# Hybrid decoder layer on one core: ScalarE takes over the remaining threshold searches, four gate tiles are made in two passes, and the attention's pools change places

## The chip, the cores and the metric

One core of one Trainium2 chip runs the kernel. The metric is the device time of one execution in microseconds (us), the median of several runs. The five engines are PE (TensorE, the matmuls), DVE (VectorE), ACT (ScalarE), POOL (GpSimd) and SP (SyncE, whose queue issues nearly all DMAs here).

## The reference

Input x is 2048 tokens by 1024 channels, float32. Cut to what matters:

```
h = rms_norm(x);  P = h @ w_in        # conv parts, q, k, v, indexer iq, ik, iw, gates g_a, g_b
y_a = (B * causal_conv3(C * x_a)) @ w_branch_a
score[t,s] = sum_h iw[t,h] * relu(iq[t,h] . ik[s])            # causal
idx = top_k(score, 256)               # per query token
y_b = softmax(q . k[idx] + bias) @ v[idx]  ->  @ w_branch_b   # 8 heads
m = sigmoid(g_a) * y_a + sigmoid(g_b) * y_b
x = x + m @ w_out
x = x + swiglu(rms_norm(x))           # 1024 -> 2816 -> 1024
out = rms_norm(x)
```

## The kernel before, in words

Matmuls in full precision are made as three: an operand is split into a high part that the fast float32 format holds and the rest, and `mm3` (L154 to L157) multiplies high by high, high by low and low by high. The tokens stand in 4 chunks of 512, or 16 blocks of 128 (blocks 0 to 7 are chunks 0 and 1).

**Stage A** makes all projections. `proj` (L187) loads the weights of one tile of 128 columns (two DMAs of 256 KB, split into whi on ScalarE, L129, and wlo on GpSimd, L130) and does 24 matmuls for each chunk, with the chunks' transposed inputs hThi and hTlo. Between them it steps a generator of indexer scores (`score`, L250): for a block of queries and up to 512 keys, per head two matmuls into sc (L258, L259), a ReLU on ScalarE into a buffer r (L261, three buffers), and a multiply-add on VectorE into acc (L266). Finished scores go to DRAM (SD). After the queries and the indexer come six gate tiles, the convolution and ten more gate tiles (`evac_gate`, L508: tanh, then a store to GT).

**The searches.** For each block of queries from block 2 on, the value of the 256th largest score is found bit by bit. On VectorE (`descend`, L298) each bit is one count over all keys of the block (`count`, L285) and two tiny steps (L339 and L341, or the like for the upper bits); there are 33 counts. On ScalarE (`descend_act`, L373) each bit is one pass of Sign with a sum over the keys (L358), and two tiny steps (way, L367; nt, L369); there are 33 passes. Then `topk` (L418) makes the mask on VectorE (L425 to L447) and stores it to DRAM (MS); the attention loads it as Mt. `A_DVE` and `A_ACT` list the blocks searched in stage A by either engine, `C_ACT` those that ScalarE searches later, between attention 0 and attention 1. All searches have low priority: the tile scheduler puts their instructions where its own simulation has the engine free, and writes one fixed order for each engine and for SP's queue.

**The halves.** `attention(half)` (L559) handles blocks 7 to 0 in half 0 and blocks 15 to 8 in half 1, four heads at a time (head groups hg 0 and 1): logits (L629, L630), a reduction on VectorE that adds mask and bias and takes the maximum (L632), the exponential (L636), transposes (L676) into ph and pl, products with V (L663, L664), then t, which is copied from PSUM on ScalarE (L668), multiplied by the spread reciprocals R on GpSimd (L669), and stored to AT (L670). Its SBUF pools stack up as kv, ap, pr. The merge follows: w_branch_a and w_branch_b are loaded (L808) and split into wab, the conv output (YT) and AT are loaded (L779, L785), the gates are loaded (L828, L830). Then come w_out (dn<-o), the norm and the transposes into h2hi and h2lo (`norm_transpose`, L839; L147 to L150), and SwiGLU (L899 on). The pools of merge and SwiGLU reuse the bytes of the attention's pools, tile by tile: a load into such a tile waits for whatever last used its bytes.

```
A_ACT, A_DVE = (5, 6, 7, 8, 9, 10), (2, 3, 4)
C_ACT, C_DVE = (15, 14, 13, 12, 11), ()
```

Of the kernel before, what the change touches and what calls it, by code (L numbers as in the profile page):

```python
# [25 lines left out]
P = 128  # L26
# [20 lines left out]

A_ACT, A_DVE = (5, 6, 7, 8, 9, 10), (2, 3, 4)
C_ACT, C_DVE = (15, 14, 13, 12, 11), ()
ORDER = ((7, 6, 5, 4, 3, 2, 1, 0), (15, 14, 13, 12, 11, 10, 9, 8))  # L50
# [24 lines left out]
def trunk_kernel(tc, x, g_mix, w_in, b_gate, conv_w, w_a, w_b, w_out, rel_bias,  # L75
# [38 lines left out]
    bg = const.tile([P, 16], F32, name="bg")  # L114
    zero = edge.tile([P, 1], F32, name="zero")
    nc.gpsimd.memset(zero, 0.0)
# [133 lines left out]
    def score(b):  # L250
        iqb = iqp.tile([P, NH, P], F32R, name="iqb", tag="iqu", bufs=2)
        c, o = divmod(b * P, CH)
        nc.gpsimd.dma_start(out=iqb, in_=IQ[c][:, :, o:o + P].rearrange("h p t -> p h t"))
        for s0, w in cut((b + 1) * P):
            acc = tk.tile([P, CH], F32, name="acc", tag="acc", bufs=2)
            for h in range(NH):
                sc = scp.tile([P, CH], F32, name="sc", tag="sc")
                nc.tensor.matmul(sc[:, 0:w], iqb[:, h, :], IKH[:, s0:s0 + w], start=True, stop=False)  # L258
                nc.tensor.matmul(sc[:, 0:w], iqb[:, h, :], IKL[:, s0:s0 + w], start=False, stop=True)  # L259
                r = tk.tile([P, CH], F32, name="r", tag="r", bufs=3)  # L260
                nc.scalar.activation(r[:, 0:w], sc[:, 0:w], AF.Relu)  # L261
                wv = iwT[:, b, h:h + 1]
                if h == 0:
                    nc.vector.tensor_scalar(acc[:, 0:w], r[:, 0:w], wv, None, op0=ALU.mult)
                else:
                    nc.vector.scalar_tensor_tensor(acc[:, 0:w], r[:, 0:w], wv, acc[:, 0:w],  # L266
                                                   op0=ALU.mult, op1=ALU.add)
                yield
            if s0 + w == (b + 1) * P:
                nc.vector.tensor_tensor(acc[:, w - P:w], acc[:, w - P:w], cmin, op=ALU.min)  # L270
            nc.sync.dma_start(out=SD[b][:, s0:s0 + w], in_=acc[:, 0:w])
        if b in A_DVE:
            select_block(b)
        elif b in A_ACT:
            select_block_act(b)
# [15 lines left out]
    def parts(b):  # L291

        for s0, w in cut((b + 1) * P):
            S = TK["p"].tile([P, CH], F32, name="S", tag="S", bufs=2)
            nc.sync.dma_start(out=S[:, 0:w], in_=SD[b][:, s0:s0 + w])
            yield slice(s0, s0 + w), w, S[:, 0:w].bitcast(U16).rearrange("p (n e) -> p n e", e=2)

# [152 lines left out]
    def select_block(b):  # L450
        with tc.high_priority(offset=-LOW):
            topk(b, descend(b), wide("J"))

    def select_block_act(b):
        with tc.high_priority(offset=-LOW):
            thr = descend_act(b)
            topk(b, thr, TK["a"].tile([P, TK["alen"]], U8, name="dump", tag="dump", bufs=1).bitcast(BF16))

# [91 lines left out]
    for ch in range(4):  # L550
        conv_tile(ch)
    for j in range(6, 16):
        proj(C_GA + j * P, P, evac_gate(j))
    for _ in scores:
        pass
# [3 lines left out]
    def attention(half):  # L559
        b_stack = ExitStack()  # L560
        LH = (half + 1) * 1024
        kvp = pool(b_stack, f"kv{half}")
        ap = pool(b_stack, f"ap{half}")
        prp = pool(b_stack, f"pr{half}")
        lgp = pool(b_stack, f"lg{half}", bufs=LGB, space=PSUM)
# [24 lines left out]
        def setup(b):  # L590
# [15 lines left out]
            near = min(lw, 2 * P)  # L606
            MBs = [ap.tile([P, CH], F32, name="MB", tag="MB", bufs=4) for _ in range(2)]
            if lw > near:
# [5 lines left out]
        def logits(st, hg, res):  # L614

            b, n, q, Mt, spans, near, MBs = st
            lw = spans[-1][1]
            sums = ap.tile([P, 4], F32, name="sums", tag="sums", bufs=3)
            for hh in range(4):
# [3 lines left out]
                pr = prp.tile([P, LH], F32, name="pr", tag="pr", bufs=PRB[half])  # L623
                mx = ap.tile([P, 5], F32, name="mx", tag="mx", bufs=6)
                for i, (s0, w) in enumerate(spans):
# [12 lines left out]
                yield  # L638
            rec = ap.tile([P, 4], F32, name="rec", tag="rec", bufs=3)
            nc.vector.reciprocal(rec, sums)  # L640
            res.append(rec)

        def spread(b, hg, rec):

            tp = tpb.tile([P, CH], F32, name="tpb", tag="tpb")
            in_order(nc.tensor.transpose(tp[0:4, 0:P], rec, ident))
            row = ap.tile([4, P], F32, name="row", tag="row", bufs=2)
            nc.scalar.copy(row, tp[0:4, 0:P])
# [95 lines left out]
    for half in (0, 1):  # L744
        ends = attention(half)
        mc = ExitStack()
        if half == 0:
            search_pool(mc, "tkc", C_DVE, C_ACT, 4)
            TK["p"].tile([P, 16], F32, name="pad")
        bigp = pool(mc, f"bigp{half}", bufs=4)  # L750
# [119 lines left out]
        if half == 0:  # L870
            with tc.issue_after(ends[-1].ins):
                for b, ba in itertools.zip_longest(C_DVE, C_ACT):
                    if ba is not None:
                        select_block_act(ba)
                    if b is not None:
                        select_block(b)
        if half == 1:
# [104 lines left out]
```

## Time and profile before

| | |
|---|---|
| median of 3 runs | 3313.43 us (3310.44 to 3317.68) |
| the profiled execution | 3308.23 us |
| its span | 3306.3 us |
| mean granted TensorE clock | 0.990 |
| PE busy | 3206.5 us, 97% |
| VectorE busy | 1744.3 us, 53% |
| ScalarE busy | 1763.8 us, 53% |
| GpSimd busy | 774.4 us, 23% |

The span is the time from the first to the last instruction that the profile shows; the execution's time has some 2 us more around it. Times inside the trace count from the span's start. A share of busy time is a mean over stages that have different limits: stage A lasts to about 1004 us, attention 0 to about 1147, SwiGLU of half 0 to about 2078, attention 1 to about 2369.

### The profile page before, as it was taken

The page shows a single profiled execution, that of the slowest core. Times are in us where ns is not written, and L with a number is a line of the kernel's source. Part 1 is how long each engine was busy: PE and PEld are TensorE (multiplying, and loading weights), DVE is VectorE, ACT ScalarE, POOL GpSimd, SP SyncE. Part 2 cuts the span into 40 slices and gives each one's busy share as a digit, 9 for nine tenths or more (in the row PEclk, how much of TensorE's full clock was granted, in tenths as well). Part 3 has the DMA queues.
Part 4 walks back from the last instruction along what each step waited for, and adds up shares of the span by engine and source line. Part 5 has one row for each costly group of instructions (what it writes and reads, how often), then busy time and mean ns, then how long its engine had stood idle before and what let it go on. Part 6 is the DMA issues. An engine that isn't in the chain of part 4 may idle for free.

```text
span 3306.3 us, 41232 instructions
## 1 busy us (share of the span) xinstructions
PE 3206.5 (97%) x14723; PEld 2626.5 (79%) x14723; DVE 1744.3 (53%) x3422; ACT 1763.8 (53%) x3250; POOL 774.4 (23%) x684
## 2 busy tenths in 40 slices
PE   8999899999997899899999999999999999999999
PEld 6777788888886678788888888787787888888887
DVE  6389756565327775554535423898854422332234
ACT  6433478877877786867586611677632211111111
POOL 5411012221013520321221222222222222212221
PEclk9999999999999999999999999999999999999999
DMA  7643333333235692322212211422571411111111
GB/s 231 179 126 115 93 97 96 92 98 107 85 99 137 167 287 78 98 78 83 88 60 77 79 51 60 115 60 72 149 250 45 147 51 44 46 51 45 45 45 51
DMA packets 347077, 328.94 MB, mean 99 GB/s; under 512 B 20596, under 2 KB 276808, under 8 KB 346488
## 3 DMA queue, kind: packets, MB, share of 16 engines
q1 hardware_dynamic: 310248, 297.84, 29.4%
q0 software_dynamic: 36624, 28.48, 4.0%
q8 instruction: 115, 1.88, 0.2%
q14 instruction: 90, 0.74, 0.1%
HBM read 252.28 MB, written 75.54 MB: 99 GB/s over the span
## 4 chain that ended last, share of the span: by engine, by line
PE 79%; DVE 9%; DMA 5%; ACT 3%; issue 2%; POOL 1%; SPq 0%; POOLq 0%; DVEq 0%; ACTq 0%
PE gu L155 11%; PE gu L157 11%; PE gu L156 11%; PE mm L157 6%; PE mm L155 6%; PE mm L156 6%; PE dn L155 5%; PE dn L157 5%; PE dn L156 5%; PE tpb L676 3%; DVE J L285 2%; PE pv L663 2%; PE lg L629 1%; PE pv L664 1%; PE lg L630 1%
## 5 line engine op out<-in xcount | busy, mean ns | idle before, releaser
L155 PE MATMUL gu<-h2hi,wgu 128*128 128x512 f32 x1408 | 552.7, 393 | 0.0
L156 PE MATMUL gu<-h2lo,wgu 128*128 128x512 f32 x1408 | 552.1, 392 | 0.0
L157 PE MATMUL gu<-h2hi,wgu 128*128 128x512 f32 x1408 | 552.0, 392 | 0.0
L358 ACT ACTIVATE dump<-key,nt 128x768 uint8<-128x768 int16 (+21 forms) x330 | 484.2, 1467 | 8.4
L157 PE MATMUL mm<-hThi,wlo 128*128 128x512 f32 (+2 forms) x1216 | 471.7, 389 | 2.6 <-POOL wlo L130 2.5
L155 PE MATMUL mm<-hThi,whi 128*128 128x512 f32 (+2 forms) x1216 | 473.7, 390 | 0.4 <-ACT whi L129 0.4
L156 PE MATMUL mm<-hTlo,whi 128*128 128x512 f32 (+2 forms) x1216 | 471.1, 388 | 0.0
L937 DVE SCALAR_TENSOR_TENSOR x<-dn,x 128x512 f32<-128x512 f32 x352 | 241.7, 689 | 224.4 <-PE dn L157 224.3
L130 POOL TENSOR_TENSOR wlo<-raw,whi 128x512 fp32r<-128x512 f32 (+1 forms) x132 | 175.9, 1333 | 696.8 <-ACT whi L129 659.3
L156 PEld LDWEIGHTS gu<-h2lo,wgu 128*128 128x128 f32 x1408 | 265.2, 188 | 58.5
L157 PEld LDWEIGHTS gu<-h2hi,wgu 128*128 128x128 f32 x1408 | 265.0, 188 | 58.6
L155 PEld LDWEIGHTS gu<-h2hi,wgu 128*128 128x128 f32 x1408 | 265.2, 188 | 58.4
L130 POOL TENSOR_TENSOR hid<-th,hid 128x512 fp32r<-128x512 f32 x88 | 114.6, 1302 | 808.1 <-ACT hid L129 800.8
L266 DVE SCALAR_TENSOR_TENSOR acc<-r,iwT,acc 128x512 f32<-128x512 f32 (+2 forms) x266 | 196.1, 737 | 197.3 <-ACT r L261 196.6
L920 DVE SCALAR_TENSOR_TENSOR th<-th,gu 128x512 f32<-128x512 f32 x88 | 60.5, 687 | 432.5 <-ACT th L919 379.0
L130 POOL TENSOR_TENSOR wgu<-raw,wgu 128x1024 fp32r<-128x1024 f32 x88 | 216.6, 2462 | 271.5 <-ACT wgu L129 268.4
L155 PE MATMUL dn<-wd,hid 128*128 128x512 f32 x704 | 274.5, 390 | 0.0
L157 PE MATMUL dn<-wd,hid 128*128 128x512 f32 x704 | 274.1, 390 | 0.0
L156 PE MATMUL dn<-wd,hid 128*128 128x512 f32 x704 | 274.0, 389 | 0.0
L157 PEld LDWEIGHTS mm<-hThi,wlo 128*128 128x128 f32 (+1 forms) x1216 | 227.1, 187 | 54.5 <-POOL wlo L130 5.1
L155 PEld LDWEIGHTS mm<-hThi,whi 128*128 128x128 f32 (+1 forms) x1216 | 227.4, 187 | 44.1 <-ACT whi L129 1.7
L156 PEld LDWEIGHTS mm<-hTlo,whi 128*128 128x128 f32 (+1 forms) x1216 | 227.4, 187 | 42.9
(229 smaller groups left out, 5853.3 us busy)
## 6 DMA issues: line engine op xcount, KB each, us to landing
raw<-in_w_in_dram SPq DMA_DIRECT2D x124, 256.0 KB
raw<-in_w_ffn_gate_dram SPq DMA_DIRECT2D x44, 512.0 KB
raw<-in_w_ffn_up_dram SPq DMA_DIRECT2D x44, 512.0 KB
raw<-in_w_ffn_down_dram SPq DMA_DIRECT2D x44, 512.0 KB
S<-SD SPq DMA_DIRECT2D x80, 256.0 KB
GT<-f SPq DMA_DIRECT2D x64, 256.0 KB
ta<-GT SPq DMA_DIRECT2D x64, 256.0 KB
S<-SD SPq DMA_DIRECT2D x68, 192.0 KB
```

What stands on the lines that cost most here:

```text
L130: lo_eng.tensor_tensor(lo, raw, hi.bitcast(F32), op=ALU.subtract)
L155: nc.tensor.matmul(ps, whi, xhi, start=start, stop=False)
L156: nc.tensor.matmul(ps, whi, xlo, start=False, stop=False)
L157: nc.tensor.matmul(ps, wlo, xhi, start=False, stop=stop)
L266: nc.vector.scalar_tensor_tensor(acc[:, 0:w], r[:, 0:w], wv, acc[:, 0:w], op0=ALU.mult, op1=ALU.add)
L285: nc.vector.tensor_scalar(wide("J")[:, 0:n], xs, thr, None, op0=op, op1=ALU.add, accum_out=cnt)
L358: nc.scalar.activation(dump, keys, AF.Sign, bias=nt, accum_out=sm)
L629: in_order(nc.tensor.matmul(lg[:, o2:e2], q[:, h, :], KH[:, s0 + o2:s0 + e2], start=True, stop=False))
L663: in_order(nc.tensor.matmul(pv, V[:, sb, :], ph, start=sb == 0, stop=False))
L676: in_order(nc.tensor.transpose(tp[:, hh * P:(hh + 1) * P], Ps[hh][:, sb * P:(sb + 1) * P], ident))
L920: nc.vector.scalar_tensor_tensor(th, th, 1.0, g, op0=ALU.add, op1=ALU.mult)
L937: nc.vector.scalar_tensor_tensor(x2[tt][:, ns], ps, 0.5, x2[tt][:, ns], op0=ALU.mult, op1=ALU.add)
```

## The change

The diff below is cut to its core; from the attention on, line numbers of the changed kernel are eight higher.

- ScalarE searches blocks 2 to 9 in stage A, and VectorE none; block 10 moves to the later group (15, 14, 13, 12, 11, 10).
- In that group block 15 may start when the attention's last ph and pl are made, and its `topk` only after the last norm transpose; all others only after the last norm transpose. Before, all of them could start at the first of these points.
- The last four gate tiles (12 to 15) are made for chunks 0 and 1, then once more loaded and made for chunks 2 and 3.
- r has four buffers, the score parts S two in stage A and four in the later group.
- The attention's pools stack up as kv, mb (MB, sums, mx), pr, ap (ph, pl, R, t), few (rec, row).

```diff
-A_ACT, A_DVE = (5, 6, 7, 8, 9, 10), (2, 3, 4)
-C_ACT, C_DVE = (15, 14, 13, 12, 11), ()
+A_ACT, A_DVE = tuple(range(2, 10)), ()
+C_ACT, C_DVE = (15, 14, 13, 12, 11, 10), ()
...
-                r = tk.tile([P, CH], F32, name="r", tag="r", bufs=3)
+                r = tk.tile([P, CH], F32, name="r", tag="r", bufs=4)
...
-            S = TK["p"].tile([P, CH], F32, name="S", tag="S", bufs=2)
+            S = TK["p"].tile([P, CH], F32, name="S", tag="S", bufs=TK["eqs"])
...
-    def select_block_act(b):
-        with tc.high_priority(offset=-LOW):
+    def select_block_act(b, after=()):
+        with tc.high_priority(offset=-LOW), ExitStack() as stack:
             thr = descend_act(b)
+            for ins in after:
+                stack.enter_context(tc.issue_after(ins))
             topk(b, thr, TK["a"].tile([P, TK["alen"]], U8, name="dump", tag="dump", bufs=1).bitcast(BF16))
...
-    for j in range(6, 16):
+    for j in range(6, 12):
         proj(C_GA + j * P, P, evac_gate(j))
+    for chunks in ((0, 1), (2, 3)):
+        for j in range(12, 16):
+            proj(C_GA + j * P, P, evac_gate(j), chunks)
...
         kvp = pool(b_stack, f"kv{half}")
+        mbp = pool(b_stack, f"mb{half}")
+        mbp.tile([P, 56], F32, name="pad")
+        prp = pool(b_stack, f"pr{half}")
         ap = pool(b_stack, f"ap{half}")
-        prp = pool(b_stack, f"pr{half}")
+        few = pool(b_stack, f"few{half}")
...
             with tc.issue_after(ends[-1].ins):
-                for b, ba in itertools.zip_longest(C_DVE, C_ACT):
-                    if ba is not None:
-                        select_block_act(ba)
-                    if b is not None:
-                        select_block(b)
+                select_block_act(C_ACT[0], [transposed[-1].ins])
+            with tc.issue_after(transposed[-1].ins):
+                for b in C_ACT[1:]:
+                    select_block_act(b)
```

What the scheduler makes of it shows in the engines' fixed order. VectorE where stage A ends and attention 0 begins (L410 to L415 end a search, L425 to L447 are its topk, L632, now L640, are the attention's reductions), before:

```order
L410 TENSOR_SCALAR li<-nt 128x1
L413 TENSOR_TENSOR li<-li,turn 128x1
L415 TENSOR_TENSOR thr<-li,top 128x1
L425 SCALAR_TENSOR_TENSOR dump,cnt_7133<-S,thr,zerob 128x512 x2
L632 ISA pr,mx<-lg,Mt 128x512
L632 ISA mx 128x1
L431 TENSOR_TENSOR more<-cnt_7133 128x1
```

and after the change:

```order
L446 SCALAR_TENSOR_TENSOR eq<-S,thr,eq 128x384
L447 TENSOR_SCALAR eq<-eq 128x384
L441 TENSOR_SCALAR eq<-S,thr 128x384
L442 SCALAR_TENSOR_TENSOR cs<-eq,last 128x384
L444 CAST last<-cs 128x1
L445 SCALAR_TENSOR_TENSOR eq<-cs,need,eq 128x384
L446 SCALAR_TENSOR_TENSOR eq<-S,thr,eq 128x384
L447 TENSOR_SCALAR eq<-eq 128x384
L640 ISA pr,mx<-lg,Mt 128x512
L640 ISA mx 128x1
```

Before, the last search's end (block 10) and the head of its topk stand ahead of the first reduction, and the rest of that topk among the reductions. Now the last topk (block 9) stands whole ahead of the first reduction, and the last pass of that block on ScalarE comes ahead of the last nine of the gates' evacuations; before, block 10's last pass came behind all of them.

SP's queue where attention 0 ends and the merge begins, before (RD, R and AT<-t belong to the attention, the raw loads and ta to the merge, S<-SD to a search):

```order
L650 DMA RD_81<-row 4x128
L808 DMA raw_12250<-in_w_branch_a_dram 128x4x128
L650 DMA RD_82<-row 4x128
L808 DMA raw_12256<-in_w_branch_b_dram 128x4x128
L652 DMA R<-RD_81 128x512
L670 DMA AT_77<-t 128x4x128
L652 DMA R<-RD_82 128x512
L670 DMA AT_77<-t 128x4x128
L828 DMA ta<-GT_114 128x512
```

and after:

```order
L660 DMA R<-RD_82 128x512
L295 DMA S<-SD_148 128x512
L678 DMA AT_77<-t 128x4x128
L295 DMA S<-SD_148 128x512
L678 DMA AT_77<-t 128x4x128
L295 DMA S<-SD_148 128x512 x2
L793 DMA raw_12218<-AT_77 64x2x512
L678 DMA AT_77<-t 128x4x128
L793 DMA raw_12218<-AT_77 64x2x512
L793 DMA raw_12219<-AT_77 64x2x512 x2
L816 DMA raw_11935<-in_w_branch_a_dram 128x4x128
L816 DMA raw_11941<-in_w_branch_b_dram 128x4x128
```

The first load of w_branch_a has moved from ahead of the attention's last four stores to behind the last of them and behind four loads from AT. The same holds at the end of attention 1.

ScalarE at the norm transposes of half 0 (o<-x squares a token tile, h2hi evacuates transposes, L358 to L369 are a search), before:

```order
L135 ACTIVATE o_13676,ss<-x_12988 128x1024
L358 ACTIVATE dump,sm<-key,start_hi 128x1920
L367 ACTIVATE way<-sm 128x1
L369 ACTIVATE nt<-way,start_hi 128x1
L358 ACTIVATE dump,sm<-key,nt 128x1920
L149 ACTIVATE h2hi<-gu 128x4x128
L135 ACTIVATE o_13698,ss<-x_13037 128x1024
L149 ACTIVATE h2hi<-gu 128x4x128 x3
```

and after:

```order
L135 ACTIVATE o_13361,ss<-x_12673 128x1024
L149 ACTIVATE h2hi<-gu 128x4x128
L135 ACTIVATE o_13383,ss<-x_12722 128x1024
L149 ACTIVATE h2hi<-gu 128x4x128 x9
L129 ACTIVATE wd<-raw_15429 128x1024
```

Block 14's search stood among the transposes' evacuations; now its first pass comes behind all sixteen. The last search of the group ends ahead of the 39th of the 44 tanh of this SwiGLU, with block 10 in it; before, the last, block 11, ended ahead of the 32nd.

## Rows read from the trace of the kernel before

**Rows 1.** The page: the chain that ended last, its share by engine.

```profile
PE 79%; DVE 9%; DMA 5%; ACT 3%; issue 2%; POOL 1%; SPq 0%; POOLq 0%; DVEq 0%; ACTq 0%
```

**Rows 2.** Busy time by stretch: stage A, its first and its later part.

```profile
core 0: us, PE busy (x) PEld busy (x) DVE busy (x) ACT busy (x) POOL busy (x), PEclk, DMA share, GB/s
180.00:420.00 240.00, 224.42 (x981) 180.70 (x980) 203.56 (x592) 95.37 (x206) 28.57 (x23) 0.99 0.38 112
420.00:960.00 540.00, 539.38 (x2409) 449.28 (x2408) 289.00 (x533) 438.22 (x984) 92.25 (x73) 1.00 0.34 98
```

**Rows 3.** Waits, 180 to 440 us: total us, times, longest.

```profile
PE sc L258 <- ACT r L261: 13.2, 11, 6.5
```

**Rows 4.** Groups by line and shape, VectorE, whole span: count, busy, mean ns.

```profile
L285 DVE TENSOR_SCALAR_CACHE_REDUCE J<-up,l 128x512 bf16<-128x512 uint16 x16 | 11.9, 744 | 0.4
...
L341 DVE SCALAR_TENSOR_TENSOR l<-l,ldrop 128x1 f32<-128x1 f32 x48 | 11.3, 235 | 1.4
...
L339 DVE TENSOR_SCALAR ldrop<-cnt,more 128x1 f32<-128x1 f32 x48 | 10.2, 212 | 1.1
```

**Rows 5.** Groups by line and shape, ScalarE, whole span.

```profile
L369 ACT ACTIVATE nt<-way,nt 128x1 f32<-128x1 f32 x330 | 96.5, 292 | 8.2
...
L358 ACT ACTIVATION_READ_ACCUMULATOR dump<-key,nt 128x1 f32 x330 | 61.8, 187 | 0.0
...
L358 ACT ACTIVATE dump<-key,nt 128x1408 uint8<-128x1408 int16 x15 | 22.0, 1468 | 0.4
...
L358 ACT ACTIVATE dump<-key,nt 128x768 uint8<-128x768 int16 x15 | 14.0, 934 | 0.4
```

**Rows 6.** Timeline of PE where stage A ends and attention 0 begins.

```profile
1004.35 0.39 PE L157 MATMUL mm<-hThi,wlo 128*128 128x512 f32 x1
...
1015.54 0.80 PE L629 MATMUL lg<-KH,q 128*128 128x512 f32 x1 [9.44 <-DVE mx L632]
```

**Rows 7.** Timeline of VectorE in the same place.

```profile
1012.75 0.15 DVE L410 TENSOR_SCALAR li<-nt 128x1 int32<-128x1 f32 x1 [39.84 <-ACT nt L369]
```

**Rows 8.** Busy time by stretch (columns as in rows 2): attention 0, attention 1.

```profile
1020.00:1060.00 40.00, 33.47 (x180) 24.86 (x179) 40.00 (x104) 30.34 (x57) 16.80 (x23) 0.99 0.31 84
...
1060.00:1100.00 40.00, 38.55 (x244) 33.26 (x243) 36.73 (x103) 34.83 (x80) 24.44 (x34) 1.00 0.45 104
...
2080.00:2100.00 20.00, 18.53 (x81) 11.15 (x81) 18.78 (x54) 16.32 (x20) 6.03 (x10) 1.00 0.32 117
```

**Rows 9.** Timeline of PE at the norm transposes, half 0, then half 1.

```profile
1339.68 0.40 PE L157 MATMUL dn<-o,mglo 128*128 128x512 f32 x1
...
1357.96 0.66 PE L155 MATMUL gu<-h2hi,wgu 128*128 128x512 f32 x1
...
2554.01 0.39 PE L157 MATMUL dn<-o,mglo 128*128 128x512 f32 x1
...
2564.68 0.78 PE L155 MATMUL gu<-h2hi,wgu 128*128 128x512 f32 x1
```

**Rows 10.** Timelines of SP's queue and of PE where attention 0 ends.

```profile
1144.09 0.38 SPq L808 DMA_DIRECT2D raw<-in_w_branch_a_dram  x1
...
1154.23 0.37 SPq L670 DMA_DIRECT2D AT<-t  x1
...
1148.52 0.80 PE L155 MATMUL gu<-y,wab 128*128 128x512 f32 x1 [3.03 <-ACT wab L129]
```

**Rows 11.** Busy time by stretch: first merge; SwiGLU of half 0.

```profile
1180.00:1200.00 20.00, 15.20 (x58) 11.73 (x56) 13.27 (x16) 16.06 (x27) 4.97 (x3) 0.83 1.04 318
...
1860.00:1980.00 120.00, 120.00 (x531) 99.30 (x530) 48.87 (x82) 31.72 (x49) 26.42 (x15) 1.00 0.22 65
```

**Rows 12.** Timelines of SP's queue and of PE where attention 1 ends.

```profile
2364.53 0.61 SPq L808 DMA_DIRECT2D raw<-in_w_branch_a_dram  x1
...
2373.09 0.37 SPq L670 DMA_DIRECT2D AT<-t  x1
...
2370.39 0.50 PE L155 MATMUL gu<-y,wab 128*128 128x512 f32 x1 [1.00 <-ACT wab L129]
```

More of the change, by code (lines that the diff above doesn't have):

```diff
@@ L114, in trunk_kernel @@
     bg = const.tile([P, 16], F32, name="bg")
-    zero = edge.tile([P, 1], F32, name="zero")
+    zero = edge.tile([P, 40], F32, name="zero")[:, 0:1]
     nc.gpsimd.memset(zero, 0.0)
@@ L606, in setup @@
             near = min(lw, 2 * P)
-            MBs = [ap.tile([P, CH], F32, name="MB", tag="MB", bufs=4) for _ in range(2)]
+            MBs = [mbp.tile([P, CH], F32, name="MB", tag="MB", bufs=4) for _ in range(2)]
             if lw > near:
@@ L617, in logits @@
             lw = spans[-1][1]
-            sums = ap.tile([P, 4], F32, name="sums", tag="sums", bufs=3)
+            sums = mbp.tile([P, 4], F32, name="sums", tag="sums", bufs=3)
             for hh in range(4):
@@ L623, in logits @@
                 pr = prp.tile([P, LH], F32, name="pr", tag="pr", bufs=PRB[half])
-                mx = ap.tile([P, 5], F32, name="mx", tag="mx", bufs=6)
+                mx = mbp.tile([P, 5], F32, name="mx", tag="mx", bufs=6)
                 for i, (s0, w) in enumerate(spans):
@@ L638, in logits @@
                 yield
-            rec = ap.tile([P, 4], F32, name="rec", tag="rec", bufs=3)
+            rec = few.tile([P, 4], F32, name="rec", tag="rec", bufs=3)
             nc.vector.reciprocal(rec, sums)
@@ L646, in spread @@
             in_order(nc.tensor.transpose(tp[0:4, 0:P], rec, ident))
-            row = ap.tile([4, P], F32, name="row", tag="row", bufs=2)
+            row = few.tile([4, P], F32, name="row", tag="row", bufs=2)
             nc.scalar.copy(row, tp[0:4, 0:P])
@@ L748, in trunk_kernel @@
             search_pool(mc, "tkc", C_DVE, C_ACT, 4)
-            TK["p"].tile([P, 16], F32, name="pad")
+            TK["p"].tile([P, 112], F32, name="pad")
         bigp = pool(mc, f"bigp{half}", bufs=4)
```

## The prediction, made before the changed kernel ran

> **What bounds the kernel now.** I read the chain that ended last first: nearly four fifths of it are PE, and VectorE has the largest other share [rows 1]. The time is PE's work plus the places where PE lacks input, so I looked for those stretch by stretch. Four are touched by this change.
>
> First, stage A. The two stretches of [rows 2] hold the same kinds of matmul. From 420 to 960 us, with ScalarE searching, PE issues 2409 matmuls in 540 us, 0.224 us each, busy throughout. From 180 to 420, where VectorE searches blocks 2 to 4, it issues 981 in 240 us; at 0.224 these need 219.9, so **20.1 us are lost**. VectorE is busy 203.56 of 240 there, ScalarE only 95.37. The waits name the link: PE's score matmuls wait for the ReLU on ScalarE that frees their PSUM buffer [rows 3], and I take that ReLU to wait in turn for VectorE, whose counts stand in front of the accumulations that free r.
>
> Second, the start of attention 0. The last projection issues at 1004.35, and after a few logits PE waits 9.44 us for the first reductions, until 1015.54 [rows 6]. VectorE was free, but its fixed order has the end of block 10's search ahead of them, which waits for ScalarE until 1012.75 [rows 7]. The rest of that topk then shares VectorE with the reductions: VectorE is busy 40 of 40 us from 1020 to 1060, and PE gets through 180 matmuls where the next 40 us hold 244 [rows 8].
>
> Third, the norm transposes of half 0, 18.3 us from the last w_out matmul to the first of SwiGLU, against 10.7 in half 1, which has no search [rows 9]. Fourth, the two places where attention gives way to the merge; there the first w_branch_a load is early, at 1144.09, and the first merge matmul follows 4.4 us later [rows 10].
>
> **The change part by part**, against the profiled execution of 3308.23 us, which lies 5.2 below the median.
>
> *A. VectorE's searches leave stage A.* Per bit VectorE loses a count and two tiny steps, for block 3 0.744 + 0.212 + 0.235 = 1.19 us [rows 4]; 99 bits for the three blocks make about 118 us, over half of the 203.56 that it is busy there. ScalarE gains 99 passes. A pass over 768 keys takes 0.934 and one over 1408 takes 1.468 [rows 5], a line of 0.83 ns a key and 0.29 us, so my estimate for 512 keys is 0.72; with the sum's readout 0.187, way and nt (0.292 each at most) 1.5 us a bit, 148 us in all. Block 10's 33 passes of 1.468 + 0.77 = 2.24 us, 74 us, leave the stage. Net, ScalarE gets 74 us more on top of 95 + 438 busy in 780 us [rows 2]; its idle time is 246. PE stands still nowhere to speak of while ScalarE is 81% busy (438 of 540), and 607 of 780 is 78%. So I take the whole loss as gained: **−20**. Bounds: 0, if the releaser is another, and −25, as the early blocks' score matmuls are narrower and should have given more than 981 a higher rate.
>
> The Trainium skill, page ScalarE: Activation LUTs, section Rules for kernel authors, speaks against this part: cheap arithmetic belongs on VectorE, which it puts at up to about three times faster per element in bf16. The rows do not bear that out for these counts: 0.744 us for 512 keys on VectorE against my 0.72 on ScalarE, so neither engine is cheaper by much. By the page, VectorE would do the same pass in a third, and the move would only load ScalarE; that outcome is rival 3 below.
>
> *B. The start of attention 0.* In the new order the last topk stands whole ahead of the first reduction and its search ends nine gate evacuations before the stage does, so reductions can start with the first logits. Of the loss, 9.44 is the wait, about 2 the stretch behind it in which a matmul shows 0.80 instead of 0.39 us [rows 6], and 64 of 244 matmuls in 40 us, 10.5, the crowded VectorE [rows 8]: 22. Some stays, since exponentials have to fill before the first transposes. Attention 1 starts with no search ahead, and its second stretch has 81 matmuls in 20 us where the rate of 244 in 40 gives 122: 6.7 us lost [rows 8]. I take **−15**, bounds −9 (the wait alone) and −22 (all).
>
> *C. Norm transposes.* Block 14's search leaves them, so half 0 should look like half 1: 18.3 − 10.7 = 7.6 [rows 9]. I take **−7**, bounds 0 and −8.
>
> *D. First merge.* The order of SP's queue puts w_branch_a behind the last AT store and four loads from AT. Such a load needs the stores before it landed. The store of the next-to-last group issued at 1154.23 before [rows 10]; with the queue free of merge loads I let it come at about 1154 again. Landing takes about what w_branch_a needed to be loaded and split, 4.4; the last store and four loads follow, some 2 us, so w_branch_a issues near 1160 and the first merge matmul near 1164.5, **16 us** later than 1148.52. Part comes back. The first merge lacks input later on as well: 1180 to 1200 holds 58 matmuls, 13.0 us of work, with the DMA engines full [rows 11]; of these 7 us I give back 6, as GT and AT tiles land in the gap. Term **+10**. Bounds +3 (w_branch_a only as late as the last t, and everything absorbed) and +18 (nothing absorbed, and splits behind block 15's passes, which now begin ahead of the first of them).
>
> *E. Second merge.* Here w_branch_a issued at 2364.53, the last AT store at 2373.09 and the first merge matmul at 2370.39 [rows 12]. Without merge work ahead the last store would come near 2371; a load 0.8 behind it gives the first matmul at 2372 + 5.9 = 2377.5, +7. I take **+5**, because this merge is short of transfers right after, bounds 0 and +10.
>
> *F. At nothing.* The second load of four gate tiles (8 DMAs, 8 splits on ScalarE, 8 on GpSimd) lies under two chunks of matmuls a tile, 48 × 0.224 = 10.8 us, with DMA at 0.34 [rows 2]; uncovered it would cost a few us for each of four tiles. Block 10's 74 us go into SwiGLU of half 0, where PE is full from 1860 to 1980 and ScalarE busy 31.72 of 120 [rows 11]; without that room its mask would hold attention 1, which needs block 10 as its sixth. The fourth r only adds slack.
>
> **Sum:** −20 − 15 − 7 + 10 + 5 = −27, so 3281 for the profiled execution and **3286 us** as a median.
>
> **The rivals.**
>
> 1. *Stage A keeps its stalls.* If the score matmuls wait for something else than VectorE's searches, A is 0: −7, 3306. For it: the named waits of PE sum to 13.2, less than the 20 lost. Against it: the stalls end where VectorE's load ends. Chance 0.13.
>
> 2. *The boundaries absorb nothing.* D at +18 and E at +10 give −14, 3299. For it: DMA is full there, and a later load has nothing to catch up with. Against it: the YT and AT tiles land meanwhile. Chance 0.16.
>
> 3. *Slower: ScalarE becomes the bound in stage A.* ReLUs stand behind passes in ScalarE's fixed order; there are now 264 passes instead of 198 in the stage, and no engine left to take the rest. The measured waits of PE for a ReLU were 13.2 / 11 = 1.2 us each [rows 3]. If one pass in ten costs that, 26 × 1.2 = +31 replaces −20, and the sum is −15 − 7 + 15 + 31 = +24, 3337. It turns slower than before when A exceeds +7, 0.03 us a pass. Against it: 198 passes cost PE next to nothing from 420 on. Chance 0.09.
>
> 4. *The reductions are still late.* If block 9's topk, ahead of the first reduction, is itself late on the chip, B is 0: −12, 3301. For it: the order is the scheduler's guess, and before the same guess was 8 us off. Against it: nine gate evacuations, 24 × 0.224 = 5.4 us apart, lie between, 48 us. Chance 0.06.
>
> 5. *More than that:* B and D at their good ends, −22 and +3: −41, 3272 or less. Chance 0.05.
>
> **How the numbers follow.** The forecast keeps 0.51; its own range is 3272 to 3299 (half of each bound's distance). The range over all is **3267 to 3306**: it takes in rivals 1, 2, 4 and most of 5, and leaves out rival 3 and tails. No change means within 0.2%, 6.6 us, about what a measurement of this kernel can tell: 3306.8 to 3320.0. Faster collects the forecast, rivals 2, 4 and 5 and half of rival 1, 0.83; same the other half and margins, 0.08; slower is rival 3, 0.09.
>
> **What would show it.** A: some 1070 matmuls from 180 to 420, VectorE well under 200 us there. B: no wait of 9 us at the first logits, and no L425 to L447 among the reductions. C: some 11 us from w_out to SwiGLU. D and E: the first w_branch_a load behind the last AT<-t, and PE idle for over 10 us ahead of the first merge matmul of half 0 and over 5 ahead of that of half 1 (3.03 and 1.00 now [rows 10, 12]). F: PE full in SwiGLU of half 0, and no wait for Mt in attention 1. I am wrong if ScalarE's waits show up on PE beyond 420 us, or if the time is over 3306.

## The result, and the profile after

The changed kernel takes 3277.84 us (median of 4 runs, 3274.26 to 3283.88) against 3313.57 for the kernel before, measured with it: a ratio of 0.9893, 95% interval 0.9873 to 0.9914. The profiled execution took 3280.84, its span is 3279.1, 27.2 less than the span before. Medians differ by more, 35.7, because the one profiled execution lies 3.0 above its median and the one before 5.3 below.

To see where the time went I cut both spans at marks that every trace here has: the last projection matmul (mm), the first and last transpose of an attention (tpb), the last matmul of a merge that reads wab, the last of w_out (dn<-o), the first and last of SwiGLU. A stage's length is the time from one mark to the next, in one execution of each kernel.

| stage | before | after | difference | forecast |
|---|---|---|---|---|
| stage A | 1004.4 | 980.2 | -24.2 | -20 (A) |
| attention 0, to its first transpose | 21.3 | 9.7 | -11.6 | -15 (B), both rows |
| attention 0, the rest | 116.7 | 115.1 | -1.6 | |
| first merge | 112.8 | 126.5 | +13.7 | +10 (D) |
| w_out, half 0 | 84.6 | 84.4 | -0.2 | 0 |
| norm transposes, half 0 | 18.3 | 9.5 | -8.8 | -7 (C) |
| SwiGLU, half 0 | 719.5 | 731.4 | **+11.9** | 0 (F) |
| attention 1 | 287.6 | 288.1 | +0.5 | 0 |
| second merge | 104.7 | 109.7 | +5.0 | +5 (E) |
| w_out and norm, half 1 | 95.0 | 95.0 | 0 | 0 |
| SwiGLU, half 1 | 733.1 | 721.1 | **-12.0** | 0 (pads) |
| the end | 8.5 | 8.6 | +0.1 | 0 |
| span | 3306.3 | 3279.1 | -27.2 | -27 |

The five terms came out within 5 us of their forecast. Two that I had costed at nothing are over 11 us each and cancel.

Busy time by stretch in the changed kernel, columns as in [rows 2], for stage A:

```profile
180.00:420.00 240.00, 240.00 (x1089) 201.26 (x1088) 108.57 (x222) 206.34 (x566) 30.99 (x26) 1.00 0.40 118
420.00:960.00 540.00, 540.00 (x2411) 450.19 (x2410) 289.76 (x519) 431.75 (x981) 104.77 (x81) 1.00 0.34 98
```

Against [rows 2], PE issues 1089 matmuls instead of 981 from 180 to 420 us and is busy all the time; VectorE is down to 108.57, ScalarE up to 206.34. The later stretch is what it was. The link that the prediction assumed, the ReLU of a score waiting for VectorE's accumulation, stands among ScalarE's waits from 180 to 440 us, before (total us, times, longest):

```profile
ACT r L261 <- DVE acc L266: 39.9, 20, 2.9
```

In the changed kernel the ReLU's largest wait there is 12.4 us for its own input from PE, and none for the accumulation is left. The first 40 us of attention 0 from about its first transposes on, before and in the changed kernel:

```profile
1025.00:1065.00 40.00, 35.09 (x201) 27.52 (x201) 39.88 (x102) 31.55 (x62) 15.22 (x21) 1.00 0.37 96
```

```profile
990.00:1030.00 40.00, 36.62 (x215) 30.73 (x213) 34.51 (x91) 32.54 (x67) 18.17 (x26) 0.96 0.33 75
```

VectorE is no longer full, but PE issues only 14 matmuls more, some 3 us of work.

The timeline of PE in the changed kernel, at the start of attention 0 and at the norm transposes:

```profile
980.21 0.39 PE L157 MATMUL mm<-hThi,wlo 128*128 128x512 f32 x1
...
982.75 0.50 PE L637 MATMUL lg<-KH,q 128*128 128x512 f32 x1 [0.17 <-DVE mx L640]
...
1315.87 0.40 PE L157 MATMUL dn<-o,mglo 128*128 128x512 f32 x1
...
1325.34 0.78 PE L155 MATMUL gu<-h2hi,wgu 128*128 128x512 f32 x1
```

The wait of 9.44 in [rows 6] has become 0.17, and the norm takes 9.5 us, a little less than the 10.7 of half 1 [rows 9]. Where attention 0 gives way to the merge, SP's queue and PE:

```profile
1113.34 0.37 SPq L678 DMA_DIRECT2D AT<-t  x1
...
1115.92 0.59 SPq L793 DMA_DIRECT2D raw<-AT  x1
1116.60 0.55 SPq L678 DMA_DIRECT2D AT<-t  x1
...
1119.16 0.59 SPq L816 DMA_DIRECT2D raw<-in_w_branch_a_dram  x1
```

```profile
1110.29 0.63 PE L672 MATMUL pv<-pl,V 128*128 128x512 f32 x1
1125.78 0.80 PE L155 MATMUL gu<-y,wab 128*128 128x512 f32 x1 [14.86 <-ACT wab L129]
```

The load of w_branch_a is now behind the last AT store and four loads from AT, and PE waits 14.86 us where it waited 3.03 [rows 10]. From the last transpose to the first merge matmul it is 20.8 us instead of 6.2. At the end of attention 1 PE waits 8.83 us where it waited 1.00 [rows 12]:

```profile
2358.14 0.79 PE L155 MATMUL gu<-y,wab 128*128 128x512 f32 x1 [8.83 <-ACT wab L129]
```

What I had not expected stands in SwiGLU of half 0. VectorE, ScalarE and PE there, in the changed kernel (L381 to L384 prepare block 13's keys, L927 and L928 make th, L358 is a pass of block 13's search):

```profile
1497.51 0.56 DVE L384 SCALAR_TENSOR_TENSOR key<-dump,key 128x384 int16<-128x384 bf16 x1
1497.99 0.68 DVE L927 SCALAR_TENSOR_TENSOR th<-th,gu 128x512 f32<-128x512 f32 x1
1498.77 0.69 DVE L928 TENSOR_TENSOR th<-gu,th 128x512 f32<-128x512 f32 x1
```

```profile
1503.06 1.79 ACT L358 ACTIVATE dump<-key,nt 128x1792 uint8<-128x1792 int16 x1
1504.76 0.19 ACT L358 ACTIVATION_READ_ACCUMULATOR dump<-key,nt 128x1 f32 x1
1504.85 0.61 ACT L129 ACTIVATE hid<-th 128x512 fp32r<-128x512 f32 x1
```

```profile
1505.52 0.80 PE L155 MATMUL dn<-wd,hid 128*128 128x512 f32 x1 [2.57 <-ACT hid L129]
1506.11 0.63 PE L156 MATMUL dn<-wd,hid 128*128 128x512 f32 x1
```

th is ready at 1499.4, but in ScalarE's fixed order three passes of the next search come ahead of hid, and PE waits for hid. After the wait a matmul shows 0.80 and 0.63 instead of 0.39, and the granted clock is at the lower of its two levels, 1.2 of 2.4 GHz, for most of the next 3.5 us. The stretch behind the wait in the changed kernel, then 1400 to 2000 us before and in the changed kernel:

```profile
1505.50:1509.00 3.50, 3.36 (x7) 2.24 (x8) 0.00 (x0) 3.40 (x7) 1.27 (x1) 0.52 0.00 0
```

```profile
1400.00:2000.00 600.00, 600.00 (x2649) 496.76 (x2648) 265.85 (x483) 359.15 (x596) 138.03 (x74) 1.00 0.24 73
```

```profile
1400.00:2000.00 600.00, 595.04 (x2606) 490.52 (x2605) 293.69 (x531) 431.19 (x734) 135.74 (x72) 0.99 0.25 75
```

So the waits cost more than their length: the 43 matmuls that are missing are 9.7 us at the rate before (600 us for 2649), of which PE stands idle for 5.0; the rest is lost at the low clock.

### The profile page after: what moved, and what is told of

Read it like the earlier page. It is cut to its first block, busy times and chain, and to the rows that moved or that the text cites. A ratio compares the mean times of both kernels' runs of the same rounds, so it can differ in the third digit from the quotient of the medians.

```text
span 3279.1 us, 41331 instructions
## 1 busy us (share of the span) xinstructions
PE 3186.7 (97%) x14723; PEld 2628.6 (80%) x14723; DVE 1668.3 (51%) x3046; ACT 1891.4 (58%) x3654; POOL 793.1 (24%) x692
## 5 line engine op out<-in xcount | busy, mean ns | idle before, releaser
L358 ACT ACTIVATE dump<-key,nt 128x384 uint8<-128x384 int16 (+27 forms) x420 | 549.0, 1307 | 10.7
L130 POOL TENSOR_TENSOR wlo<-raw,whi 128x512 fp32r<-128x512 f32 (+1 forms) x140 | 187.9, 1343 | 672.7 <-ACT whi L129 593.0
L927 DVE SCALAR_TENSOR_TENSOR th<-th,gu 128x512 f32<-128x512 f32 x88 | 60.4, 686 | 390.4 <-ACT th L926 353.1
```

The costliest lines, as they stand in the source:

```text
L130: lo_eng.tensor_tensor(lo, raw, hi.bitcast(F32), op=ALU.subtract)
L358: nc.scalar.activation(dump, keys, AF.Sign, bias=nt, accum_out=sm)
L927: nc.vector.scalar_tensor_tensor(th, th, 1.0, g, op0=ALU.add, op1=ALU.mult)
```

## The experiments

Stage lengths by the same marks, in us of the profiled execution (attention 1 with its start); medians and ratios against the kernel before, measured along with each. The runs were made at different times, and the median of the kernel before lay between 3310.01 and 3314.25 in them, so runs of different groups are best compared by their ratios (e1 to e4, e5 to e8, e9 and e10, e11 and e12 were measured together).

| run | stage A | start att. 0 | merge 0 | norm 0 | SwiGLU 0 | att. 1 | merge 1 | SwiGLU 1 | median | ratio, 95% interval |
|---|---|---|---|---|---|---|---|---|---|---|
| before | 1004.4 | 21.3 | 112.8 | 18.3 | 719.5 | 287.6 | 104.7 | 733.1 | 3313.57 | |
| changed | 980.2 | 9.7 | 126.5 | 9.5 | 731.4 | 288.1 | 109.7 | 721.1 | 3277.84 | 0.9893 (0.9873 to 0.9914) |
| e1 | 979.6 | 12.0 | 127.9 | 9.2 | 737.2 | 287.8 | 112.5 | 733.6 | 3302.68 | 0.9965 (0.9953 to 0.9976) |
| e2 | 980.2 | 9.7 | 111.4 | 18.4 | 719.8 | 287.9 | 106.7 | 733.5 | 3277.63 | 0.9887 (0.9872 to 0.9901) |
| e3 | 980.3 | 10.4 | 117.5 | 9.0 | 729.1 | 292.7 | 106.8 | 719.5 | 3265.15 | 0.9853 (0.9838 to 0.9868) |
| e4 | 980.7 | 10.9 | 120.3 | 9.5 | 743.5 | 287.6 | 109.0 | 719.5 | 3289.27 | 0.9923 (0.9908 to 0.9938) |
| e5 | 979.9 | 10.2 | 126.0 | 8.6 | 730.8 | 287.8 | 109.7 | 719.9 | 3280.36 | 0.9899 (0.9885 to 0.9914) |
| e6 | 979.6 | 10.4 | 127.1 | 13.5 | 730.3 | 288.1 | 108.2 | 718.9 | 3284.87 | 0.9915 (0.9898 to 0.9931) |
| e7 | 981.0 | 10.2 | 126.5 | 9.6 | 731.3 | 288.4 | 108.2 | 718.7 | 3277.82, one run | |
| e8 | 980.2 | 11.6 | 112.5 | 9.3 | 731.6 | 292.6 | 105.7 | 719.6 | 3267.22 | 0.9859 (0.9844 to 0.9874) |
| e9 | 980.7 | 9.7 | 127.7 | 8.6 | 722.4 | 287.8 | 111.5 | 718.5 | 3271.39 | 0.9882 (0.9865 to 0.9898) |
| e10 | 979.9 | 9.7 | 112.5 | 9.4 | 732.5 | 293.1 | 104.9 | 719.5 | 3263.95 | 0.9858 (0.9843 to 0.9872) |
| **e11** | 980.3 | 9.7 | 113.4 | 9.5 | 725.5 | 289.3 | 104.4 | 718.2 | **3252.19** | **0.9827 (0.9810 to 0.9843)** |
| e12 | 980.4 | 9.7 | 126.3 | 9.5 | 730.2 | 287.9 | 108.1 | 719.4 | 3273.68 | 0.9890 (0.9875 to 0.9905) |

**e1: the tile zero at its old size.**

```diff
-    zero = edge.tile([P, 40], F32, name="zero")[:, 0:1]
+    zero = edge.tile([P, 1], F32, name="zero")
```

> The changed kernel with the one-column tile named zero back at its old size, so that everything on the right side of SBUF stands 128 bytes higher: wgu starts at 192 modulo 256 bytes in both halves, h2hi and h2lo stay at 64. In the kernel before this was so in half 1 alone, where gate and up matmuls issued every 0.231 us instead of 0.227. Theory (the place decides): 0.231 us in SwiGLU of both halves, 11 to 12 us more in each, about 3301 in all. Rival (the slower spacing was a matter of that execution, or of a transfer beside it): 0.227 in both, 3278.

SwiGLU of half 1 goes back to 733.6, and the whole is 25 us longer. The costliest gate and up groups, by line (count, busy us, mean ns): in half 0 of the kernel before, 1400 to 2000 us, then in half 1, 2600 to 3200 us, in the kernel before, the changed kernel and e1.

```profile
L155 PE MATMUL gu<-h2hi,wgu 128*128 128x512 f32 x581 | 226.0, 389 | 0.0
```

```profile
L155 PE MATMUL gu<-h2hi,wgu 128*128 128x512 f32 x578 | 228.2, 395 | 0.0
```

```profile
L155 PE MATMUL gu<-h2hi,wgu 128*128 128x512 f32 x578 | 224.8, 389 | 0.0
```

```profile
L155 PE MATMUL gu<-h2hi,wgu 128*128 128x512 f32 x576 | 227.6, 395 | 0.0
```

A matmul shows longer than the interval to the next start, but the 6 ns stand in the intervals too: the mean of those under 0.3 us between gate and up matmuls is 0.2326 us in half 1 before and 0.2325 in both halves of e1, and 0.2267 in half 0 before and in both halves of the changed kernel. SwiGLU of half 0 got only 5.8 us longer although its matmuls slowed as much; PE's waits for hid on ScalarE are not there in e1, presumably since a slower PE gives ScalarE the time. The theory of the place holds (e7 tells whether 192 itself or the difference costs), its sum for half 0 did not.

**e2: the lists alone**, in the kernel before.

```diff
-A_ACT, A_DVE = (5, 6, 7, 8, 9, 10), (2, 3, 4)
-C_ACT, C_DVE = (15, 14, 13, 12, 11), ()
+A_ACT, A_DVE = tuple(range(2, 10)), ()
+C_ACT, C_DVE = (15, 14, 13, 12, 11, 10), ()
```

> The kernel before with the two lists of blocks changed and nothing else (VectorE searches none, block 10 searched later); pools, gates, pads, r and S as before. Theory (the lists alone give the gains in stage A and at the start of attention 0): -24 and -13 in those two, nothing lost where attention gives way to the merge, SwiGLU of half 1 at the old 0.231 spacing: 3276, between 3270 and 3285 as the searches fall otherwise in SwiGLU of half 0. Rival (the early start of attention 0 needs the gates' two passes and the pools' new order): -24 alone, 3289.

These two lines give the whole gain: -24.2 in stage A, -11.6 at the start of attention 0, everything else as before within 2 us, and the changed kernel's median. By the medians all the rest of the change together is worth nothing: by stages it gains 8.9 at the norms and 12.4 in SwiGLU 1 and loses 15.1 in the first merge, 3 in the second and 11.6 in SwiGLU 0. These stages sum to a loss of 8.4, because the profiled execution of e2 lies 5.2 below its median and that of the changed kernel 3.0 above.

**e3: the pools' old order** in the changed kernel.

```diff
         mbp.tile([P, 56], F32, name="pad")
-        prp = pool(b_stack, f"pr{half}")
         ap = pool(b_stack, f"ap{half}")
         few = pool(b_stack, f"few{half}")
+        prp = pool(b_stack, f"pr{half}")
```

> The changed kernel with the attention's ph, pl, R, t, rec and row below pr again (kv, mb, ap, few, pr). w_branch_a is then queued ahead of the last AT stores as before. Theory (the pools' order costs the two merges their early loads and gives nothing else): first merge 14 us shorter, second 5, start of attention 0 unchanged: 3278 - 19 = 3259. Rival (the order pays for itself at the start of attention 0): that start gives back up to 13: 3272.

SP's queue in e3:

```profile
1106.19 0.39 SPq L816 DMA_DIRECT2D raw<-in_w_branch_a_dram  x1
...
1119.53 0.37 SPq L678 DMA_DIRECT2D AT<-t  x1
```

w_branch_a is 13 us ahead of the last AT store, the first merge matmul comes 6.2 after the last transposes, and the first merge is 9 us shorter, the second 3 (14 and 5 were expected), the whole 13. The start of attention 0 hardly moves (10.4), so the new order does not pay for itself there. Attention 1 is 4.6 longer; e8 shows that pr's place is not the reason.

**e4: two S buffers.**

```diff
-            S = TK["p"].tile([P, CH], F32, name="S", tag="S", bufs=TK["eqs"])
+            S = TK["p"].tile([P, CH], F32, name="S", tag="S", bufs=2)
```

> The changed kernel with two S buffers everywhere. Theory (with four, a block's keys are prepared among the topk of the block before, VectorE then makes th late, ScalarE has begun the next block's passes, and hid stands behind them: the two stalls of PE ahead of dn at 1502 and 1638 us): SwiGLU of half 0 without these two, about 10 us less, 3268. Rival (the stalls come from how many searches stand in that SwiGLU, not from the buffers): two or more such stalls stay, 3278.

My theory fell, with the sign against it: SwiGLU of half 0 is 12 longer still. VectorE, and PE behind it:

```profile
1500.69 0.43 DVE L381 TENSOR_SCALAR key<-S 128x512 uint16<-128x512 uint16 x1 [2.19 <-DMA S<-SD]
...
1504.91 0.68 DVE L928 TENSOR_TENSOR th<-gu,th 128x512 f32<-128x512 f32 x1
```

```profile
1507.48 0.80 PE L155 MATMUL dn<-wd,hid 128*128 128x512 f32 x1 [4.84 <-ACT hid L129]
```

With two buffers the key preparation waits for its loads, and th, queued behind it on VectorE, is made 6 us later. Four buffers shorten the change of blocks (the end of one search with its topk, and the keys of the next); they are not the cause of the loss.

**e5: blocks 14 to 10 released later.**

```diff
-            with tc.issue_after(transposed[-1].ins):
-                for b in C_ACT[1:]:
-                    select_block_act(b)
...
+                    if half == 0 and fpair == 0 and tt == 0 and n == 0:
+                        with tc.issue_after(upd.ins):
+                            for b in C_ACT[1:]:
+                                select_block_act(b)
```

> The changed kernel with blocks 14 to 10 released by the first down-projection's update of SwiGLU half 0 instead of the last norm transpose: every change from one block's search to the next then falls into the stretch in which PE works on the down-projection, where hid is not wanted at once, instead of right ahead of it. Theory (the stalls of SwiGLU half 0 are a matter of where in its cycle of 65 us a search ends): no wait of dn for hid over 1 us, SwiGLU of half 0 at 720 to 722 instead of 731.4, 3268 in all. Rival (ScalarE has too many searches in that SwiGLU wherever they start): such waits stay, 3275 to 3279.

**e6: all released where attention 0 ends, as before.**

```diff
             with tc.issue_after(ends[-1].ins):
-                select_block_act(C_ACT[0], [transposed[-1].ins])
-            with tc.issue_after(transposed[-1].ins):
-                for b in C_ACT[1:]:
+                for b in C_ACT:
                     select_block_act(b)
```

> The changed kernel with all later searches released where attention 0 ends, as before. Theory (holding block 14 back gains 9 us at the norm transposes, and by its shift of the searches costs 11.6 in SwiGLU): norms 18 instead of 9.5 us, SwiGLU of half 0 about 720 to 722 as before and as with the lists alone: 3276 to 3278. Rival (the SwiGLU loss has another cause, four S buffers or the pools): norms 18, SwiGLU still 731: 3287.

Both leave SwiGLU of half 0 at 730 to 731, and both expectations missed. But the waits moved. In e5, then in e6:

```profile
1907.86 0.80 PE L155 MATMUL dn<-wd,hid 128*128 128x512 f32 x1 [4.73 <-DVE x L941]
```

```profile
1577.95 0.79 PE L155 MATMUL dn<-wd,hid 128*128 128x512 f32 x1 [4.01 <-ACT hid L129]
```

In e5 no wait for hid is left, as its expectation had it, but PE waits for x, VectorE's update that frees a buffer of the down-projection. That update stands behind a change of blocks that began with the end of block 11's search at 1883.4, 12 us ahead of the down-projection; VectorE in e5:

```profile
1905.40 0.68 DVE L925 TENSOR_TENSOR th<-gu,th 128x512 f32<-128x512 f32 x1
1906.00 0.73 DVE L446 SCALAR_TENSOR_TENSOR eq<-S,thr,eq 128x512 bf16<-128x512 f32 x1
1906.66 0.54 DVE L384 SCALAR_TENSOR_TENSOR key<-dump,key 128x384 int16<-128x384 bf16 x1
1907.13 0.68 DVE L941 SCALAR_TENSOR_TENSOR x<-dn,x 128x512 f32<-128x512 f32 x1
```

So a change of blocks can hold PE up by either engine: by the passes ahead of hid on ScalarE, or by the mask and the keys ahead of th and x on VectorE. Shifting all searches by one amount only moved the changes of blocks; some again fell at the end of a gate and up stretch (in e6, block 12's first pass at 1570.5, the down-projection at 1573). A search takes about two of SwiGLU's cycles of 65 us, so if one change falls badly, others do. In e2 the changes fall inside or behind a down-projection (first pass of block 13 at 1458.9, the down-projection from 1428.6) and PE waits for nothing in this SwiGLU. That left the place of the changes to be told apart from the number of searches and the four buffers by e9.

**e7: both operands moved.** e1, and

```diff
+    const.tile([P, 32], F32, name="lpad")
     zerob = const.tile([P, 1], BF16, name="zerob")
```

> The changed kernel with zero at its old size and a tile of 128 bytes ahead of the left side's pools, so that weights and inputs of nearly every matmul start at 192 modulo 256 bytes, both of them. Theory (what costs is that the two operands differ modulo 256): 0.2265 us for gate and up matmuls, 721 in SwiGLU of half 1, as in the changed kernel. Rival (192 itself costs): 0.2325, 733, and stage A some 2% longer too, near 1000.

SwiGLU of half 1 takes 718.7, and gate and up matmuls are back at 389 ns (lines are one higher here):

```profile
L156 PE MATMUL gu<-h2hi,wgu 128*128 128x512 f32 x579 | 225.2, 389 | 0.0
```

So 192 is no worse than 64; what costs is that weights and inputs start at different places, 128 bytes apart modulo 256.

**e8: e3 with e5 and pr at 64.**

```diff
         few = pool(b_stack, f"few{half}")
+        few.tile([P, 40], F32, name="pad2")
+        prp = pool(b_stack, f"pr{half}")
```

> The changed kernel with the pools' old order as in e3, a pad that puts pr at 64 modulo 256, and the release of e5. Theory (the costs are independent): e3's 3265 less 10 in SwiGLU of half 0 and less 3 to 5 in attention 1, whose start and middle were 5 us longer in e3, where pr stood at 160: 3251, between 3246 and 3257. Rival (attention 1 in e3 was longer by the pools' order itself): 3255 and attention 1 as in e3.

It is no better than e3: SwiGLU 0 keeps its waits as in e5, and attention 1 its 292.6. The rival was right on attention 1.

**e9: searches paced by the down-projections** in the changed kernel. Search and topk become two functions, and

```diff
+                    if half == 0 and fpair % 2 == 0 and tt == 0 and n == 0:
+                        with tc.issue_after(upd.ins):
+                            while late:
+                                mask_act(*late.pop())
+                            if todo:
+                                b = todo.pop(0)
+                                late.append((b, search_act(b)))
```

> The changed kernel with the searches of SwiGLU half 0 paced: each of blocks 14 to 10 is started, and the topk of the block before is made, at the first update of every second down-projection (fpair 0, 2, 4, 6, 8, 10). In the changed kernel, e5 and e6 the change of blocks fell 0 to 18 us ahead of a down-projection, in the kernel before and e2 within or behind one. Theory (that place is what costs): no wait of dn over 1 us in SwiGLU of half 0, 720 to 722 us instead of 731, 3268 in all. Rival (six searches there, or the four S buffers, cost it wherever the changes fall): 729 to 732, 3278.

PE's waits in SwiGLU of half 0, changed kernel and e9:

```profile
PE dn L155 <- ACT hid L129: 4.1, 2, 2.6
PE dn L155 <- DVE x L944: 0.9, 1, 0.9
PE dn L157 <- POOL hid L130: 0.6, 1, 0.6
```

```profile
PE dn L155 <- DVE x L948: 2.8, 1, 2.8
```

and the stretch from 1400 to 2000, which holds 2606 matmuls in the changed kernel, in e9:

```profile
1400.00:2000.00 600.00, 600.00 (x2649) 496.99 (x2648) 267.35 (x501) 437.88 (x745) 135.28 (x74) 1.00 0.24 73
```

With as many searches and buffers, SwiGLU of half 0 takes 722.4. One wait is left, where the last block's topk is made. With the searches and buffers unchanged and only their place moved, the waits for hid are gone: the place of the change of blocks is shown as the cause. For the whole kernel the gain is small: the ratios of e9 and of the changed kernel have overlapping intervals.

**e10 and e11: the lists, the pacing of e9 and aligned operands** in the kernel before, with its pools and gates; e11 with four S buffers as well. The pads:

```diff
-    zero = edge.tile([P, 1], F32, name="zero")
+    zero = edge.tile([P, 40], F32, name="zero")[:, 0:1]
...
+        ap.tile([P, 32], F32, name="pad2")
...
-            TK["p"].tile([P, 16], F32, name="pad")
+            TK["p"].tile([P, 48], F32, name="pad")
```

> The kernel before (its pools, gates, r and S) with the lists of e2, the pacing of e9 and three pads that put all matmul operands at 64 modulo 256. Theory (the gains and costs found so far are independent): e2's 3278 less 9 at the norm transposes, less 12 to 13 in SwiGLU of half 1 and 0 to 3 in the attentions: 3255, between 3249 and 3260. Rival (the pacing costs SwiGLU of half 0 what it saves at the norms): 3265.

> e10 with four S buffers in the later group, as e9 has them. Theory (with two, the loads of S hold up VectorE at each change of blocks, which made e10's stalls ahead of the down-projections and its late start of attention 1): SwiGLU of half 0 at 720 to 723 instead of 732.5, the start of attention 1 at 14 instead of 19: 3264 - 15 = 3249, between 3245 and 3254. Rival (e10's stalls come from its pools): 3260 to 3265.

e10 has e4's trouble: two S buffers, changes of blocks that outlast the down-projection by more (block 13's first pass comes 15 us behind its end, in e11 8), 732.5. e11 has SwiGLU at 725.5 with one wait of 2.9, a little over the 720 to 723 expected, and takes 3252.19: 57.8 us less than the kernel before beside it, where the changed kernel had 35.7.

**e12: the gate tiles in one pass** in the changed kernel.

```diff
-    for j in range(6, 12):
+    for j in range(6, 16):
         proj(C_GA + j * P, P, evac_gate(j))
-    for chunks in ((0, 1), (2, 3)):
-        for j in range(12, 16):
-            proj(C_GA + j * P, P, evac_gate(j), chunks)
```

> The changed kernel with the gate tiles made in one pass for all four chunks, as before. Theory (the two passes give nothing, since e2 starts attention 0 as early without them): stage A near 980, the start of attention 0 near 10, 3278 in all. Rival (with the new pools, whose first pr tile lies where chunk 1 was, the start needs them): the start of attention 0 5 to 12 us longer, 3283 to 3290.

Nothing is lost, neither in stage A nor at the start of attention 0.

## Why the prediction was right, and where it was wrong

*The forecast*, 3286 as a median, missed by 8, inside its range; the sum of terms, -27 on the profiled execution, met the 27.2 measured, partly by luck: the misses of A and D offset each other, and so do the two effects of 12 us that had no term.

*A* was right in mechanism and a little short: -24.2 against -20, near the bound of -25 that I gave for the narrow score matmuls of the early blocks. The ReLU's wait for VectorE and PE's wait for the ReLU are gone, so rival 1 is refuted, and rival 3 for stage A too: ScalarE is busy 206 of 240 us there without PE waiting.

*B*: -13.2 against -15. The wait is gone as argued (0.17 us instead of 9.44), and e2 and e12 show that the lists alone do it. The crowded VectorE was worth less than the 10.5 that I put at it: beside the wait only 3.9 came back, and how much of that is due to the crowding is not told apart.

*C*: -8.8 against -7, a little past the bound of -8.

*D* failed in one step: "of these 7 us I give back 6". The first merge matmul came 14.6 us later than before, counted from the last transposes, close to the 16; the merge ended 13.7 later. Of the delay 0.9 was absorbed, so rival 2's mechanism was right for this merge. *E* was right at +5.0: the first matmul came 8.1 later, and 3.1 were absorbed.

*F* failed at "Block 10's 74 us go into SwiGLU of half 0, where PE is full": I named room on ScalarE in a mean over 120 us as the cover, and never asked where in SwiGLU's cycle a change of blocks falls. It cost 11.9. Block 10 itself was not the reason; in e2 it is there and costs nothing. Rival 3 had the mechanism (an urgent evacuation behind a pass, in ScalarE's fixed order) and looked for it in the wrong stage.

*The pads* had no term at all. They are three tiles whose sizes look like nothing: mb's pad, and two that the diff ahead of the prediction leaves out, zero (1 column, now 40) and the pad of the later searches' pool (16 columns, now 112). SwiGLU of half 1 gained 12.0; e1 shows that zero's size decides it, and the other two were not undone by themselves. The rows to see it were in the trace before: the same gate and up matmuls at 389 ns in half 0 and 395 in half 1.

What stays open: why attention 1 is some 5 us longer in e3, e8 and e10 (in e10 nearly all of it lies ahead of the first transposes, in e3 and e8 some 2), and why e3's first merge is 6 longer than e2's, where e8, with e3's order of pools, has 112.5. Neither was tried further.

## What to carry to other kernels

A kernel whose matrix engine is 97% busy can still lose in places, and a bundle of edits can hide that one edit gives all the gain: undo the parts one by one. When background work is put into "free" time of an engine with a fixed order, ask where its handovers fall in the foreground's cycle, not how much idle time there is; pace it by an event of that cycle, with buffers enough that the handover ends in time (e10 against e11). When two stretches run the same instructions at different mean times, look for the difference before adding terms.

## What the runs showed of the hardware

The issue interval of a matmul depended on where its two operands start: 0.2267 us (worked out as under e1) with weights and inputs at the same place modulo 256 bytes (64 and 64, or 192 and 192), 0.2325 to 0.2326 with weights at 192 and inputs at 64, at a granted clock of 1.00 from 2600 to 3200 us. The places are those of the programs' memory plans, which the traces do not hold; other distances were not tried, so that 256 is the period is not shown. The Trainium skill, page TensorE: Matmul & The Clock Gate, section Step-by-step: what each phase is for, says that the next tile's weight load takes no SBUF read bandwidth from the running matmul. Here the pair of addresses matters by 2.6%. That the two reads meet would be one reading of it; no run shows where the 6 ns are spent.

An instruction of VectorE on S took several times as long beside one of GpSimd's splits. In e5, VectorE and GpSimd:

```profile
1495.33 2.64 DVE L441 TENSOR_SCALAR eq<-S,thr 128x512 bf16<-128x512 f32 x1 [0.75 <-DMA S<-SD]
...
1499.07 0.47 DVE L441 TENSOR_SCALAR eq<-S,thr 128x512 bf16<-128x512 f32 x1
```

```profile
1495.29 2.39 POOL L130 TENSOR_TENSOR wgu<-raw,wgu 128x1024 fp32r<-128x1024 f32 x1 [3.27 <-ACT wgu L129]
```

The first ends 0.3 us behind GpSimd's split, the second has no split beside it. The Trainium skill, page GPSIMD Engine Reference, section Specifications, names an SBUF interface that the two engines share; these rows agree. A change of blocks with such splits beside it gets longer by this.

A Sign pass over 512 keys took 0.719 us on ScalarE (the estimate was 0.72), a count over as many on VectorE 0.744 [rows 4].
